# Four 32-partition transposes of mixer B's diagonal blocks made into one 128-partition transpose, before and after the substitution

## The chip, the cores and the metric

The kernel runs on one core of a Trainium2 chip. The metric is device time in microseconds of one execution, as the median of several runs. All arithmetic of this kernel is in 32-bit floats.

## What is computed

The program is one inference step of a two-layer hybrid backbone for 128 context tokens and 1024 latent tokens. Layer 0 has windowed attention (mixer A) beside a bidirectional RWKV-7 recurrence (mixer B), layer 1 has differential attention (mixer C). The change lies in mixer B alone. Its recurrence, for each of 8 heads and both directions, is

```python
def rwkv_scan(S0, r, decay, kk, a, k, v, reverse):
    def step(S, inp):
        r_t, w_t, kk_t, a_t, k_t, v_t = inp
        sa = jnp.einsum('bhvk,bhk->bhv', S, -kk_t)
        S = (S * w_t[:, :, None, :] + sa[..., None] * (kk_t * a_t)[:, :, None, :]
             + v_t[..., None] * k_t[:, :, None, :])
        return S, jnp.einsum('bhvk,bhk->bhv', S, r_t)
    ...
```

The kernel does not step through tokens. It cuts the sequence into chunks of 64 tokens. Inside a chunk the term with `sa` couples each token to the earlier ones, which makes a unit triangular 64x64 system; its inverse is needed before the chunk's state update can be done with matrix products.

## The kernel before

**Items.** Mixer B's work is cut into nine items (`items`): two halves of the latent tokens for each of four pairs of heads, and one item for the context tokens of all heads. An item holds 32 triangular systems of 64x64: two directions, eight chunks and two heads. Of each system the matrix `za` is stored with partitions as rows. Along the free axis lie 16 systems (`units`, index `u`), and an index `a` (0 or 1) tells the two chunks of a pair apart, one of which lies on the lower and one on the upper 64 partitions.

**Inverse.** A 64x64 triangular matrix is seen as four 32x32 blocks. The two diagonal blocks are inverted by substitution (`b_subst`), the off-diagonal block then follows from two small matrix products (`b_invert`). The 128 partitions hold four groups `g` of 32 partitions; group `g` holds a diagonal block that begins at column `32 * (g % 2)`, so groups 0 and 2 have it at column 0 and groups 1 and 3 at column 32.

- `b_subst` first turns each diagonal block, so that columns of all systems lie side by side (`mp`, 128 x 32 x 32), with one VectorE transpose per group (L1032, four of 32 x 1024, each element written twice). Then GpSimd does 31 steps of a multiplication (L1039, into `tmp`) and an addition (L1041, into `rp`). `rp` starts as the identity, loaded by a DMA on SP's queue (L1028).
- `b_invert` turns `rp` back into `Rt` with four VectorE transposes (L1050, 32 x 512), turns the first diagonal block once more into `rt11` (an `hb` buffer) with two transposes (L1056, 32 x 512), and then TensorE multiplies (L1061: `hb` by `za` into `sc`; ScalarE L1063 copies the result; L1068 multiplies by `Rt`; ScalarE L1070 copies into `Rt`). With `Rt` complete, TensorE makes `pa` (L1082), VectorE scales it to `E` (L1086), and L1096 and ScalarE L1099 prepare `VU`.

**Scan.** `b_scan` steps through eight chunk positions of an item, and each step waits for the one before: TensorE L1139 (`E` by `G`), VectorE L1141 (`VU`), TensorE L1143, VectorE L1150 (`G`, two instructions), ScalarE L1152 (`S`).

**Pipeline over items.** One turn of the loop over `items` (a stage here) does, interleaved, the scan of item i, the inverse of item i+1, the front part of item i+2 in both directions (`b_front`: TensorE L988, L998, L1013; VectorE `za` L1004 and `q` L1006), the substitution of item i+2 near the end, and the preparation of item i+3 (`b_prep`: VectorE L930 to L954, ScalarE L921 to L957, TensorE L914). The modulation of later parts (`mod_chunks`: TensorE L287 and L293, ScalarE L289) fills in. In every second stage the finish of a pair of heads is added (`b_finish`, L1176 to L1206). `timeline` sets when each of them is issued, and

```python
            timeline((scan, 8, *t[0]), (invert(i + 1), 8, *t[1]), (done, 10, *t[2]),
                     (front(i + 2, 0), 12, *t[3]), (prep(i + 2, 1), 5, *t[4]), (front(i + 2, 1), 12, *t[5]),
                     (subst(i + 2), 2, *t[6]), (prep(i + 3, 0), 5, *t[7]), (some(mod, t[8]), max(t[8], 1), *t[9]))
```

from that order a scheduler with costs of its own makes one fixed order for each engine. Every engine runs its instructions in that order, and an instruction that waits holds up all behind it. `mp`, `rp` and `Rt` exist once; `hb` is a ring of eleven buffers. `behind` only adds an order, that `Rt` is written after the neighbours' last use, and no wait.

Of the kernel before, what the change touches and what calls it, by code (L numbers as in the profile page):

```python
# [19 lines left out]
P = 128  # L20
# [121 lines left out]
def hybrid_step(ctx: ExitStack, tc: tile.TileContext, I, O, stop=99):  # L142
    nc = tc.nc
    PE, VE, AE, GE, SP = nc.tensor, nc.vector, nc.scalar, nc.gpsimd, nc.sync
    def behind(ins, others):

        for o in others:
            if o is not None:
                tc.add_manual_dep(ins.ins, o.ins.name, mybir.DependencyInfo(
                    mybir.DependencyClass.NoSync, mybir.DependencyReason.DATA), reason="order")  # L150

    def space(name, bufs, **kw):
        return tc.tile_pool(name=name, bufs=bufs, reuse_waits="tile", **kw)
# [3 lines left out]
    def tl(pool, shape, tag, dt=F32, bufs=None):  # L157
        uid[0] += 1
        kw = {} if bufs is None else {"bufs": bufs}
        return pool.tile(list(shape), dt, tag=tag, name=f"{tag}_{uid[0]}", **kw)  # L160
# [679 lines left out]
    ON_VE = ()  # L840
# [35 lines left out]
    low, high = (lambda j: slice(64 * j, 64 * j + 32)), (lambda j: slice(64 * j + 32, 64 * j + 64))  # L876
# [141 lines left out]
    def units(it):  # L1018
        return [it.za[:, a].rearrange("p d x h t -> p (d x h) t") for a in range(2)]

    def b_subst(it, pre, eye, eng):

        mp, rpb = tl(pre, [P, 32, 32], "mp"), tl(pre, [P, 16, 32], "rp")
        tmp = tl(pre, [P, 136], "tmp")
        za = units(it)
        SP.dma_start(rpb.rearrange("p t i -> p (t i)"), eye)  # L1028
        for g in range(4):
            s = slice(32 * g, 32 * g + 32)  # L1030
            m = za[1 - g // 2][s, :, 32 * (g % 2):32 * (g % 2) + 32].rearrange("p u c -> p c u")
            VE.transpose(mp[s].rearrange("p c i -> p (c i)"),  # L1032
                         m.rearrange("p c (o u) -> p c o u", o=1).to_broadcast([32, 32, 2, 16]))
        yield
        for j in range(31, 0, -1):
            t = j // 2
            n = 16 - t
            tv = tmp[:, :n * j].rearrange("p (t i) -> p t i", i=j)
            eng.tensor_tensor(tv, mp[:, j:j + 1, 0:j].to_broadcast([P, n, j]),  # L1039
                             rpb[:, t:16, j:j + 1].to_broadcast([P, n, j]), ALU.mult)  # L1040
            eng.tensor_tensor(rpb[:, t:16, 0:j], rpb[:, t:16, 0:j], tv, ALU.add)  # L1041
        it.rpb = rpb

    def b_invert(it, Rt, pool, pre, ps_s, ps_a):

        rpb, za = it.rpb, units(it)
        for g in (0, 2, 1, 3):
            s = slice(32 * g, 32 * g + 32)
            o = 32 * (g % 2)
            behind(VE.transpose(Rt[s, :, o:o + 32].rearrange("p u (c o) -> p c o u", o=2),  # L1050
                                rpb[s].rearrange("p c i -> p (c i)")),
                   [getattr(n, "tail", None) for n in it.near])
        it.free = True
        rt11, v1 = hb(pool, [P, 16, 32]), hb(pool, [P, 16, 32])
        for e in range(2):
            VE.transpose(rt11[low(e)], Rt[low(e), :, 0:32])  # L1056
        yield
        pv = tl(ps_s, [P, 16, 32], "sc")
        for u in range(16):
            for e in range(2):  # L1060
                PE.matmul(pv[high(e), u], za[1 - e][low(e), u, 32:64], rt11[low(e), u], start=True, stop=True)  # L1061
        for e in range(2):
            AE.copy(v1[high(e)], pv[high(e)])  # L1063
        yield
        pv = tl(ps_s, [P, 16, 32], "sc")
        for u in range(16):
            for e in range(2):
                PE.matmul(pv[low(e), u], v1[high(e), u], Rt[high(e), u, 32:64], start=True, stop=True)  # L1068
        for e in range(2):
            AE.copy(Rt[low(e), :, 32:64], pv[low(e)])  # L1070
        yield
        De = tl(pre, [P, 2, 8], "De")
        VE.memset(De, -0.5)
        w = 1 if it.nl == 1 else 2
        VE.tensor_scalar(De[:, :, 1:8:w], it.D[:, :, 0:7:w], -0.5, None, op0=ALU.mult)

        it.E = tl(pool, [P, 2, 8, 64], "E", bufs=2)
        pe = tl(ps_a, [P, 2, 2, 4, 64], "pa")
        for d in range(2):
            for x in range(4):  # L1080
                for h, e in ((0, 0), (1, 1), (0, 1), (1, 0)):
                    PE.matmul(pe[half_of(h), e, d, x], it.zn[half_of(e), d, x, half_of(h)],  # L1082
                              Rt[half_of(e), 8 * d + 2 * x + h], start=True, stop=True)
            yield
        for e in range(2):
            VE.tensor_tensor(it.E[:, :, e:8:2].rearrange("p d x t -> p (d x) t"),  # L1086
                             pe[:, e].rearrange("p d x t -> p (d x) t"),
                             De[:, :, 1 - e:8:2].rearrange("p d (x o) -> p (d x) o", o=1).to_broadcast([P, 8, 64]),
                             ALU.mult)
        yield  # L1090
        for d in range(2):
            pt = tl(ps_s, [P, 4, 2, 64], "sc")
            for x in range(4):
                for h in range(2):
                    for e in range(2):
                        PE.matmul(pt[half_of(e), x, h], Rt[half_of(e), 8 * d + 2 * x + h],  # L1096
                                  it.av[half_of(e), d, x, half_of(h)], start=True, stop=True)
            for e in range(2):
                AE.copy(it.VU[half_of(e), :, d, 1 - e], pt[half_of(e)].rearrange("p x h v -> p x (h v)"))  # L1099
            yield  # L1100
# [109 lines left out]
    with ExitStack() as ph2:  # L1210
        bc = ph2.enter_context(space("bc", 1))
        pool = ph2.enter_context(space("bpool", 1))
# [5 lines left out]
        pre = early.enter_context(space("bpre", 1))  # L1218
# [4 lines left out]
        hb = lambda pl, shape: tl(pl, shape, "hb", bufs=NHB)  # L1223
        ones, cen, ma = load_cst(bc, "ones", "cen", "ma")
        eye = I["cst"][:, CST["eye"][0]:sum(CST["eye"])]
        ind = ones[:, 0:P:64]
        Rt = tl(pre, [P, 16, 64], "Rt")
# [14 lines left out]
        items = []  # L1242
# [30 lines left out]
            return b_front(items[i], d, pool, pre, ps_y, ps_a, ma) if i < len(items) else None  # L1273

        def subst(i):
            return b_subst(items[i], pre, eye, VE if i in ON_VE else GE) if i < len(items) else None

        def invert(i):
            if not 0 <= i < len(items):
                return None  # L1280
            items[i].near = [items[j] for j in (i - 1, i + 1) if 0 <= j < len(items)]
            return b_invert(items[i], Rt, pool, pre, ps_s, ps_a)
# [22 lines left out]
        for i in range(-2, len(items)):  # L1305
            scan, tail = None, None
            if i == -1:
                blk.__exit__(None, None, None)
            if i >= 0:
                it = items[i]  # L1310
                scan = scan_all(it)
                tail = b_finish(it, pool, ps_s, ones, cen, ind) if it.last else None
# [25 lines left out]
            if i + 1 == len(items):  # L1338
                timeline((after(scan, tail), 21, 0, 1), (some(outs, 9), 9, *T8))
                continue  # L1340
# [3 lines that stand above are left out]
            done = tail  # L1344
    if stop <= 2:
# [442 lines left out]
```

## Time and profile before

| what | value |
|---|---|
| median of three runs | 2371.25 us (2370.67 to 2379.9) |
| the profiled execution | 2364.72 us, span 2362.9 us |
| mean granted TensorE clock | 0.919 |
| mixer B's items in the trace | first `mp` transpose at 609.9 us, last `Rt` transpose at about 1221 us |
| DVE line L1032, 36 transposes | 69.6 us busy, 1934 ns each |
| DVE line L1050, 36 transposes | 37.8 us busy, 1049 ns each |
| DVE line L1056, 18 transposes | 12.6 us busy, 701 ns each |
| POOL lines L1039 and L1041, 279 each | 128.0 and 133.8 us busy |

The page gives the busy time of each engine, the same in 40 slices, and groups of instructions. A row of the timeline gives the start, the duration, engine, line, operation, output and inputs, the count, and in brackets how long the engine stood still before it and what ended the wait. A row of the windows gives, for a stretch of time, the busy time of each engine with its instructions, then the clock granted to TensorE (1 is full speed), the share of the DMA engines and GB/s.

### The profile page before, as it was taken

How to read it: one execution, taken by the hardware profiler on the slowest of the kernel's cores; microseconds unless marked ns; L12 is line 12 of the kernel's file. 1: busy time of each engine (PE TensorE's matmuls, PEld its weight loads, DVE VectorE, ACT ScalarE, POOL GpSimd, SP SyncE). 2: the span in 40 equal slices, each digit the busy share in tenths (PEclk: the TensorE clock that was granted, in tenths of full speed). 3: DMA queues.
4: the chain of work that ended last, by engine and by line, in shares of the span. 5: the costliest groups of instructions: out<-in, count | busy, mean ns of one | idle time of the engine just before them, and what ended most of it. 6: DMA issues, size and time to landing. Idle time of an engine off the chain costs nothing. (4 is left out here: it accounts for less than half of the span.)

```text
span 2362.9 us, 40947 instructions
## 1 busy us (share of the span) xinstructions
PE 2109.9 (89%) x15258; PEld 1864.3 (79%) x15258; DVE 1556.2 (66%) x3838; ACT 1044.5 (44%) x2808; POOL 644.1 (27%) x897
## 2 busy tenths in 40 slices
PE   7899989997578888987899789999999999998798
PEld 4899988996456666776677678899989899997676
DVE  4445555445566676775755985778887878887743
ACT  3433334333343343352434445545555565555621
POOL 0222212310433344542240431222222122211212
PEclk9999999998877887795889899999999999999799
DMA  6421213102543243333145533011010100101233
GB/s 262 138 74 65 79 53 111 64 32 92 156 124 96 83 133 113 118 115 87 62 141 185 187 135 104 19 34 35 18 52 23 31 27 26 40 13 59 72 105 116
DMA packets 164648, 205.73 MB, mean 87 GB/s; under 512 B 16193, under 2 KB 107745, under 8 KB 164449
## 3 DMA queue, kind: packets, MB, share of 16 engines
q1 hardware_dynamic: 161584, 198.25, 26.5%
q10 hardware_dynamic: 2864, 4.85, 0.6%
q8 instruction: 121, 1.98, 0.4%
q14 instruction: 79, 0.64, 0.1%
HBM read 152.32 MB, written 50.74 MB: 86 GB/s over the span
## 5 line engine op out<-in xcount | busy, mean ns | idle before, releaser
L1493 ACT ACTIVATE p<-s,mx 128x384 f32<-128x384 f32 (+1 forms) x400 | 224.8, 571 | 128.3 <-DVE mx L1490 105.1
L1488 DVE TENSOR_REDUCE mc<-s 128x1 f32<-128x384 f32 x384 | 205.3, 551 | 37.0 <-PE s L1486 33.3
L1039 POOL TENSOR_TENSOR tmp<-mp,rp 128x126 f32<-128x126 f32 (+22 forms) x279 | 128.0, 459 | 342.6 <-DVE mp L1032 281.6
L352 PE MATMUL ps<-wch,hh 128*128 128x384 f32 x576 | 207.2, 361 | 15.3 <-DVE hh L1638 13.8
L1486 PE MATMUL s<-kst,qs 128*128 128x384 f32 x768 | 203.0, 365 | 18.6 <-ACT p L1493 17.9
L353 PE MATMUL ps<-wcl,hh 128*128 128x384 f32 x576 | 199.7, 347 | 5.1 <-POOL wcl L261 5.1
L354 PE MATMUL ps<-wch,hl 128*128 128x384 f32 x576 | 198.1, 344 | 3.0 <-DVE hl L1639 2.7
L366 PE MATMUL ps<-hh,wgh 128*128 128x384 f32 x504 | 174.6, 347 | 5.8 <-DVE bo L234 5.6
L367 PE MATMUL ps<-hl,wgh 128*128 128x384 f32 x504 | 173.7, 345 | 0.0
L368 PE MATMUL ps<-hh,wgl 128*128 128x384 f32 x504 | 172.8, 343 | 0.0
L399 POOL TENSOR_TENSOR q<-ropea,ropeb 128x256 f32<-128x256 f32 x56 | 42.9, 766 | 450.8 <-DVE ropeb L396 285.1
L1486 PEld LDWEIGHTS s<-kst,qs 128*128 128x128 f32 x768 | 131.2, 196 | 37.2 <-ACT p L1493 29.9
L261 POOL TENSOR_TENSOR wgl<-raw,wgh 128x1024 fp32r<-128x1024 f32 (+1 forms) x37 | 72.9, 1971 | 277.3 <-ACT wgh L260 261.9
L1041 POOL TENSOR_TENSOR rp<-rp,tmp 128x126 f32<-128x126 f32 (+22 forms) x279 | 133.8, 480 | 21.9
L352 PEld LDWEIGHTS ps<-wch,hh 128*128 128x128 f32 x576 | 111.1, 193 | 21.0 <-issue 12.1
L1370 DVE TENSOR_TENSOR al<-pt,ah 128x512 fp32r<-128x512 f32 (+2 forms) x168 | 100.7, 615 | 36.9 <-ACT ah L1369 35.6
L1369 ACT CAST ah<-pt 128x512 fp32r<-128x512 f32 (+2 forms) x168 | 86.4, 533 | 83.4 <-PE pt L1524 82.8
L353 PEld LDWEIGHTS ps<-wcl,hh 128*128 128x128 f32 x576 | 111.2, 193 | 7.6 <-POOL wcl L261 6.9
L354 PEld LDWEIGHTS ps<-wch,hl 128*128 128x128 f32 x576 | 110.7, 192 | 5.2 <-DVE hl L1639 4.8
L261 POOL TENSOR_TENSOR wcl<-raw,wch 128x512 fp32r<-128x512 f32 x48 | 63.3, 1327 | 161.3 <-ACT wch L260 161.3
L1524 PE MATMUL pt<-cst,p 128*128 128x128 f32 x584 | 98.4, 283 | 8.6 <-DVE p L1506 4.3
L366 PEld LDWEIGHTS ps<-hh,wgh 128*128 128x128 f32 x504 | 96.5, 192 | 7.9 <-DVE bo L234 6.2
(411 smaller groups left out, 5927.4 us busy)
## 6 DMA issues: line engine op xcount, KB each, us to landing
hb<-pbT SPq DMA_DIRECT2D x90, 256.0 KB, 4.4
adaw<-in_ada_w_dram SPq DMA_DIRECT2D x64, 256.0 KB, 3.4
raw<-in_wc_dram SPq DMA_DIRECT2D x48, 256.0 KB, 2.8
adaw<-in_ada_w_dram SPq DMA_DIRECT2D x8, 1024.0 KB, 11.9
pbT<-bm SPq DMA_DIRECT2D x16, 512.0 KB, 2.7
low<-lowT SPq DMA_DIRECT2D x16, 512.0 KB, 4.8
raw<-in_wo_dram SPq DMA_DIRECT2D x32, 256.0 KB, 2.8
raw<-in_wpb_dram SPq DMA_DIRECT2D x13, 512.0 KB, 3.5
```

The costliest lines, as they stand in the source:

```text
L261: eng.tensor_tensor(lo[:, j:j + w], raw[:, :w], hi[:, j:j + w].bitcast(F32), ALU.subtract)
L352: PE.matmul(ps[:, :n], hh[:, k, s], wh[:, k], start=k == 0, stop=False)
L353: PE.matmul(ps[:, :n], hh[:, k, s], wl[:, k], start=False, stop=False)
L354: PE.matmul(ps[:, :n], hl[:, k, s], wh[:, k], start=False, stop=k == KT - 1)
L366: PE.matmul(ps[:, :THIRD], wh[:, k], hh[:, k, s], start=k == 0, stop=False)
L367: PE.matmul(ps[:, :THIRD], wh[:, k], hl[:, k, s], start=False, stop=False)
L368: PE.matmul(ps[:, :THIRD], wl[:, k], hh[:, k, s], start=False, stop=k == KT - 1)
L1039: eng.tensor_tensor(tv, mp[:, j:j + 1, 0:j].to_broadcast([P, n, j]), rpb[:, t:16, j:j + 1].to_broadcast([P, n, j]), ALU.mult)
L1041: eng.tensor_tensor(rpb[:, t:16, 0:j], rpb[:, t:16, 0:j], tv, ALU.add)
L1486: PE.matmul(s[c][:, :w], qs[:, e, z], hd.kp[:, z] if own else hd.kst[:, z, w * c:w * c + w], start=e == 0, stop=e == 1)
L1488: VE.tensor_reduce(mc[:, c:c + 1] if nb > 1 else mx, s[c][:, :w], axis=AX.X, op=ALU.min)
L1493: AE.activation(e[:, w * c:w * c + w], s[c][:, :w], AF.Exp, scale=-1.0, bias=mx, accum_out=sums[:, z, c:c + 1])
```

## The change

`b_subst` gets the item's buffer pool and takes one more `hb` buffer, `dg`. Four copies on the engine of the substitution (GpSimd for every item, as `ON_VE` is empty) bring the four diagonal blocks to column 0; one VectorE transpose of 128 x 1024 then makes `mp`. `b_invert` turns all of `rp` with one VectorE transpose of 128 x 512 into columns 32 to 63 of `Rt`, makes `rt11` with one transpose over all partitions, and lets ScalarE copy the first diagonal block from there to columns 0 to 31 on the two groups that have it. Line numbers behind this place fall by three (L1061 becomes L1058, L1139 becomes L1136 and so on).

```diff
-    def b_subst(it, pre, eye, eng):
+    def b_subst(it, pool, pre, eye, eng):
...
+        dg = hb(pool, [P, 16, 32])
         for g in range(4):
             s = slice(32 * g, 32 * g + 32)
-            m = za[1 - g // 2][s, :, 32 * (g % 2):32 * (g % 2) + 32].rearrange("p u c -> p c u")
-            VE.transpose(mp[s].rearrange("p c i -> p (c i)"),
-                         m.rearrange("p c (o u) -> p c o u", o=1).to_broadcast([32, 32, 2, 16]))
+            eng.tensor_copy(dg[s], za[1 - g // 2][s, :, 32 * (g % 2):32 * (g % 2) + 32])
+        VE.transpose(mp.rearrange("p c i -> p (c i)"),
+                     dg.rearrange("p (o u) c -> p c o u", o=1).to_broadcast([P, 32, 2, 16]))
...
-        for g in (0, 2, 1, 3):
-            s = slice(32 * g, 32 * g + 32)
-            o = 32 * (g % 2)
-            behind(VE.transpose(Rt[s, :, o:o + 32].rearrange("p u (c o) -> p c o u", o=2),
-                                rpb[s].rearrange("p c i -> p (c i)")),
-                   [getattr(n, "tail", None) for n in it.near])
-        it.free = True
+        behind(VE.transpose(Rt[:, :, 32:64].rearrange("p u (c o) -> p c o u", o=2), rpb.rearrange("p c i -> p (c i)")),
+               [getattr(n, "tail", None) for n in it.near])
         rt11, v1 = hb(pool, [P, 16, 32]), hb(pool, [P, 16, 32])
+        VE.transpose(rt11.rearrange("p u c -> p (u c)"), Rt[:, :, 32:64])
         for e in range(2):
-            VE.transpose(rt11[low(e)], Rt[low(e), :, 0:32])
+            AE.copy(Rt[low(e), :, 0:32], Rt[low(e), :, 32:64])
```

The scheduler also gives the work around it another order. Three places follow. The first is VectorE's order for item 2's `Rt` (from `rp_7102`) and item 3's `mp` (`mp_7779`); `VU` and `G` are scan steps, `za` and `q` belong to the front of item 3, `E` to the inverse of item 2. Before:

```order
L1050 STREAM_TRANSPOSE Rt_5573<-rp_7102 32x32x16 x4
L1056 STREAM_TRANSPOSE hb_7502<-Rt_5573 32x512 x2
L978 SCALAR_TENSOR_TENSOR hb_7508<-hb_7438,rkh_5536,hb_7304 128x512
L1141 TENSOR_TENSOR VU_6017<-VU_6017,sc_7520 64x2x128
...
L1006 TENSOR_TENSOR q_1300_7506<-pa_7678,cstones_5571 128x2x4x64
L1141 TENSOR_TENSOR VU_6017<-VU_6017,sc_7733 64x2x128
L1032 STREAM_TRANSPOSE mp_7779<-za_7327 32x1024 x2
L1150 TENSOR_TENSOR G_957_5576<-S_960_5579,sc_7733 64x2x64 x2
L1122 TENSOR_TENSOR y_6602<-y_6602,yb_7519 128x256 x2
L1032 STREAM_TRANSPOSE mp_7779<-za_7327 32x1024 x2
L1086 TENSOR_TENSOR E_7698<-pa_7699,De_7695 128x8x64
```

With the change:

```order
L1048 STREAM_TRANSPOSE Rt_5573<-rp_7102 128x32x16
L1138 TENSOR_TENSOR VU_6019<-VU_6019,sc_7520 64x2x128
L1051 STREAM_TRANSPOSE hb_7501<-Rt_5573 128x512
L978 SCALAR_TENSOR_TENSOR hb_7508<-hb_7440,rkh_5536,hb_7310 128x512
...
L1006 TENSOR_TENSOR q_1303_7506<-pa_7678,cstones_5571 128x2x4x64
L1138 TENSOR_TENSOR VU_6019<-VU_6019,sc_7733 64x2x128
L1033 STREAM_TRANSPOSE mp_7779<-hb_7783 128x1024
L1147 TENSOR_TENSOR G_957_5576<-S_960_5579,sc_7733 64x2x64 x2
L1119 TENSOR_TENSOR y_6604<-y_6604,yb_7519 128x256 x2
L1083 TENSOR_TENSOR E_7698<-pa_7699,De_7695 128x8x64 x2
```

The scan's `VU` has moved ahead of the `rt11` transpose, and the whole `mp` transpose, which now waits for GpSimd's copies, stands ahead of the scan's `G`.

The second is TensorE's order at the inverse of the same item 2 (`sc_7540` is its first product, `sc_7520` a scan step, `py_7584` modulation, `pa_7575` the front of item 3). Before:

```order
L998 MATMUL pa_7575<-zr_1286_7393,kbt_7396 128x128 x4
L287 MATMUL py_7584<-adaw_7580,sc_64 2x128 x4
L287 MATMUL py_7584<-adaw_7582,sc_64 2x128 x4
L998 MATMUL pa_7575<-zr_1286_7393,kbt_7396 128x128
L1061 MATMUL sc_7540<-hb_7502,za_6648 32x32
L998 MATMUL pa_7575<-zr_1286_7393,kbt_7396 128x128 x2
L1061 MATMUL sc_7540<-hb_7502,za_6648 32x32 x31
L998 MATMUL pa_7575<-zr_1286_7393,kbt_7396 128x128
L1143 MATMUL sc_7520<-VU_6017,kb_1062_6022 128x128
```

With the change:

```order
L998 MATMUL pa_7575<-zr_1289_7395,kbt_7398 128x128 x4
L1140 MATMUL sc_7520<-VU_6019,kb_1063_6024 128x128
L1140 MATMUL sc_7520<-VU_6019,kb_1101_6188 128x128
L1058 MATMUL sc_7540<-hb_7501,za_6650 32x32 x32
L287 MATMUL py_7584<-adaw_7580,sc_64 2x128 x4
L287 MATMUL py_7584<-adaw_7582,sc_64 2x128 x4
L998 MATMUL pa_7575<-zr_1289_7395,kbt_7398 128x128 x4
```

The scan's product stands first now, and the eight modulation products that stood ahead of the inverse stand behind it.

The third is VectorE's order at item 0's `mp`, where nothing is scanned yet (L930 to L954 prepare item 1):

```order
-L1032 STREAM_TRANSPOSE mp_5917<-za_5648 32x1024 x4
 L930 TENSOR_SCALAR hb_5908<-hb_5908 128x512
-L934 MEMSET hb_5987 128x8
+L934 MEMSET hb_5989 128x8
 L301 TENSOR_SCALAR gcol_77<-py_5914,prm_60 128x2
...
+L954 TENSOR_TENSOR kbt_5997<-hb_6001,hb_5908 128x4x2x64
+L1033 STREAM_TRANSPOSE mp_5917<-hb_5921 128x1024
```

Here the transpose has moved behind the instructions that prepare item 1, L930 to L954. On GpSimd each item's four copies stand right ahead of its substitution; nothing else moves there. The order of layer 1 is the same as before on every engine.

More of the change, by code (lines that the diff above doesn't have):

```diff
@@ L1275, in subst @@
         def subst(i):
-            return b_subst(items[i], pre, eye, VE if i in ON_VE else GE) if i < len(items) else None
+            return b_subst(items[i], pool, pre, eye, VE if i in ON_VE else GE) if i < len(items) else None
         def invert(i):
```

## Prediction

> **What bounds the kernel now.** I read the page first.
>
> ```profile
> span 2362.9 us, 40947 instructions
> ...
> PE 2109.9 (89%) x15258; PEld 1864.3 (79%) x15258; DVE 1556.2 (66%) x3838; ACT 1044.5 (44%) x2808; POOL 644.1 (27%) x897
> ...
> PEclk9999999998877887795889899999999999999799
> ```
>
> TensorE (PE) is busy 89% of the span, so elsewhere a faster VectorE (DVE) is worth nothing. But slices 10 to 21, of 59 us each, are mixer B, and there the granted clock falls to 0.7 and 0.5. So I read that part apart, from 590 to 1260 us: first the groups of the changed lines, then the waits.
>
> ```profile
> L1032 DVE STREAM_TRANSPOSE mp<-za 32x1024 f32<-32x1024 f32 x36 | 69.6, 1934 | 0.4
> ...
> L1050 DVE STREAM_TRANSPOSE Rt<-rp 32x512 f32<-32x512 f32 x36 | 37.8, 1049 | 42.3 <-POOL rp L1041 41.6
> ...
> L1056 DVE STREAM_TRANSPOSE hb<-Rt 32x512 f32<-32x512 f32 x18 | 12.6, 701 | 0.5
> ...
> L1063 ACT COPY hb<-sc 32x512 f32<-32x512 f32 x18 | 10.4, 577 | 46.0 <-PE sc L1061 45.8
> ```
>
> ```profile
> POOL tmp L1039 <- DVE mp L1032: 281.6, 8, 39.9
> ...
> DVE Rt L1050 <- POOL rp L1041: 41.6, 5, 18.5
> ...
> PE sc L1061 <- DVE hb L1056: 32.5, 8, 8.1
> ```
>
> GpSimd (POOL) starts its substitution when `mp` is done; DVE then waits for its last addition (41.6 us, five times) and PE for the `rt11` transpose (32.5 us, eight times). So POOL, 27% busy over all, sits in a ring: `mp`, substitution, `Rt`, `rt11`, PE, `za`, `mp`. The timelines show one turn, from item 2's `Rt` to item 3's substitution; first DVE.
>
> ```profile
> 789.71 4.21 DVE L1050 STREAM_TRANSPOSE Rt<-rp 32x512 f32<-32x512 f32 x4 [6.30 <-POOL rp L1041]
> 793.95 1.43 DVE L1056 STREAM_TRANSPOSE hb<-Rt 32x512 f32<-32x512 f32 x2
> ...
> 813.81 0.75 DVE L1004 TENSOR_TENSOR za<-pa,cstones 128x256 f32<-128x256 f32 x2
> ...
> 815.08 0.40 DVE L1141 TENSOR_TENSOR VU<-VU,sc 64x256 f32<-64x256 f32 x1
> 815.41 3.93 DVE L1032 STREAM_TRANSPOSE mp<-za 32x1024 f32<-32x1024 f32 x2
> 819.35 0.58 DVE L1150 TENSOR_TENSOR G<-S,sc 64x128 f32<-64x128 f32 x2
> ...
> 820.75 3.93 DVE L1032 STREAM_TRANSPOSE mp<-za 32x1024 f32<-32x1024 f32 x2
> ```
>
> Then PE and POOL:
>
> ```profile
> 784.78 1.91 PE L287 MATMUL py<-adaw,sc 128*2 128x128 f32 x16
> 786.61 0.49 PE L998 MATMUL pa<-zr,kbt 64*128 64x128 f32 x2
> 794.70 0.31 PE L1061 MATMUL sc<-hb,za 32*32 32x32 f32 x2 [7.60 <-DVE hb L1056]
> ...
> 798.23 1.22 PE L1143 MATMUL sc<-VU,kb 128*128 128x128 f32 x4
> ...
> 812.36 0.71 PE L1143 MATMUL sc<-VU,kb 128*128 128x128 f32 x4
> ```
>
> ```profile
> 789.15 0.22 POOL L1039 TENSOR_TENSOR tmp<-mp,rp 128x16 f32<-128x16 f32 x1
> 789.45 0.23 POOL L1041 TENSOR_TENSOR rp<-rp,tmp 128x16 f32<-128x16 f32 x1
> 824.81 0.24 POOL L1039 TENSOR_TENSOR tmp<-mp,rp 128x31 f32<-128x31 f32 x1 [35.14 <-DVE mp L1032]
> ```
>
> POOL ends at 789.68, `Rt` and `rt11` take 5.7 us, PE resumes at 794.70 after 7.60 us, `za` ends at 814.56, `mp` at 824.68, 10.1 us behind it. POOL stood 35.14 us. Whatever shortens `za` to `mp`, or POOL to PE, shortens the turn if nothing else ends last. I put the nine items in two classes. Items 1, 2, 4 and 6 are like this one (POOL ends, DVE waiting). At items 3, 5 and 7 a pair's finish fills DVE and PE as well.
>
> **`mp`.** Four transposes of 1.93 us leave, one comes, of the same free length on 128 partitions. All 36 rows of its line have 32 partitions, so the trace bounds a transpose of 128 only from 1.93 us (partitions side by side) to 7.7 us (one after another, which would undo the change). In the rows above `VU` takes 0.40 us with 64x256 and the two `za` of 128x256 take 0.75, so DVE's time goes by the free length and not by the partitions; I take 1.93. Ahead stand four POOL copies of 512 elements on 32 partitions, an operation the trace doesn't have. The nearest rows:
>
> ```profile
> L1240 POOL MEMSET rmask<- 128x512 f32 x1 | 0.5, 524 | 0.0
> ...
> L261 POOL TENSOR_TENSOR wcl<-raw,wch 128x512 fp32r<-128x512 f32 x48 | 63.3, 1327 | 161.3 <-ACT wch L260 161.3
> ```
>
> A copy reads one input, a memset none and the subtraction two. With 0.08 us between POOL instructions (789.15 + 0.22 is 789.37, the next starts at 789.45), four cost 2.4 us by the memset and 5.6 by the subtraction. I take 0.62 each, near the memset, so 2.8; with 1.94 for the transpose and 0.2 for handing over, `za` to `mp` becomes 5.0 us (4.5 to 7.7). Its value before, by the start of `za` and the end of `mp`, for items 1 and 7 at the ends of the spread:
>
> ```profile
> 678.46 0.76 DVE L1004 TENSOR_TENSOR za<-pa,cstones 128x256 f32<-128x256 f32 x2 [0.92 <-PE pa L998]
> ...
> 679.73 7.63 DVE L1032 STREAM_TRANSPOSE mp<-za 32x1024 f32<-32x1024 f32 x4
> ...
> 1092.96 0.76 DVE L1004 TENSOR_TENSOR za<-pa,cstones 128x256 f32<-128x256 f32 x2
> ...
> 1103.52 3.88 DVE L1032 STREAM_TRANSPOSE mp<-za 32x1024 f32<-32x1024 f32 x2
> ```
>
> That is 8.1 and 13.7 us; the same reading gives 9.2, 10.1, 10.4, 12.6, 9.2 and 10.5 for items 2 to 6 and 8, of which 7.7 is transposes and the rest `G`, `y` and `E` between them. The whole transpose stands ahead of these now. So items 1, 2, 4, 6 gain 36.9 − 20.0 = 16.9 us, items 3 and 5 gain 22.7 − 10.0 = 12.7. Item 7's inverse is reached late, after POOL has long ended, so of its 8.7 I count 4; item 8's last stage is PE's, 1 of 5.5.
>
> [...]
>
> **`Rt` and `rt11`.** 4.21 + 1.43 us become 1.05 + 0.70, and PE can be 3.9 us earlier on paper. The order takes it back in the first class: the eight L287 products and the L998, in which PE worked until 787.1, stand behind the inverse now, and the scan's `VU` and L1140 stand ahead. PE's work is the same, PE is idle until POOL ends either way, and the moved products (half of the sixteen L287 that took 1.91, and 0.49) lengthen the path to `za` by 1.4, more at the low clock, while `Rt`, `VU` and `rt11` together take 2.2 us where 5.7 stood, 3.5 less, of which the scan's product L1140, now ahead, takes some 0.7 to 1.2 (L1143). What is left, about 1 us, is within what PE's own order can give or take; I count 0 for these four, bounds −2 to +2 each. In the second class `VU` stood behind it all:
>
> ```profile
> 860.56 1.07 DVE L1050 STREAM_TRANSPOSE Rt<-rp 32x512 f32<-32x512 f32 x1
> ...
> 867.18 0.42 DVE L1141 TENSOR_TENSOR VU<-VU,sc 64x256 f32<-64x256 f32 x1
> ...
> 867.66 0.71 PE L1143 MATMUL sc<-VU,kb 128*128 128x128 f32 x4 [2.23 <-DVE VU L1141]
> ```
>
> PE's 2.23 us go, and what is late next is PE's own work; three such stages give 6.9, say 7. ScalarE's two added copies (0.58 each, by L1063) run while it waits for L1061 (45.8 us): nothing; were that cover gone, 1.2 us an item, as L1065 (L1068 before) needs `Rt` complete. L1028's DMA on SP waits for the readers of the buffers as before, none of it moved past another queue; the `dg` buffer takes one of eleven `hb` slots, and I see no wait for one.
>
> **Item 0.** Its `mp` stands behind the preparation of item 1 now:
>
> ```profile
> 609.88 7.71 DVE L1032 STREAM_TRANSPOSE mp<-za 32x1024 f32<-32x1024 f32 x4
> 617.62 0.43 DVE L930 TENSOR_SCALAR hb<-hb 128x512 f32<-128x512 f32 x1
> ...
> 622.73 0.77 DVE L954 TENSOR_TENSOR kbt<-hb,hb 128x512 f32<-128x512 f32 x1
> ```
>
> L930 to L954 take 5.9 us. From 609.9, `mp` ends at 617.7 with these and its own 1.93, against 617.6, and later if one of them waits where now it doesn't: up to 3 us. POOL then makes DVE wait the full 18.5 us for `Rt`. I count −2 (−3 to +1).
>
> **Sum.** 16.9 + 12.7 + 4 + 1 + 7 − 2 = 39.6, say 40 us: 2364.72 of the profiled execution becomes 2325. The median of the runs shown is 6.5 above that execution, so I forecast 2371.25 − 40 = 2331. With all bounds at once: copies at 5.6 take 8 × 2.8 = 22 from it, the −2 four times 8 more, item 0 one more, leaving 9; the good ends (copies 3, `Rt` 8, item 0 3, item 7 5) make 59. This case's own range is 2312, with all the good ends, to 2347, with half of the bad ones.
>
> **Rivals.** *B, the clock comes back too.* The stretches of item 2's turn:
>
> ```profile
> 747.30:815.40 68.10, 54.98 (x653) 44.58 (x652) 42.81 (x77) 26.16 (x71) 29.14 (x62) 0.82 0.33 98
> ...
> 788.00:792.00 4.00, 0.00 (x0) 0.00 (x0) 2.23 (x3) 0.00 (x0) 1.28 (x6) 0.88 0.04 11
> 796.00:800.00 4.00, 4.00 (x67) 3.37 (x64) 1.77 (x6) 1.15 (x2) 0.00 (x0) 0.50 0.94 267
> ```
>
> PE stood through 788 to 792 and right after had a clock of 0.50, at which L1143 took 1.22 us against 0.71. A stage of 68 us at 0.82 loses 68 × 0.18 = 12 us of full clock; if a good third of it, 4.4 us, came back in each of eight stages, 35 us more: 2296. Against it: the second class fell to half speed behind a wait of only 2.23 us, so a short wait is no cure, and the first class's idle still reaches until POOL ends, whose wait stays.
>
> [...]
>
> *C, PE's fixed order is late next.* PE is busy 54.98 of those 68.10 us, so a turn cannot lose more than 13 us without PE's being the end of it, and PE's order was made for other durations than these. If its rows for the next front come 2.6 us later than I think in eight stages, half of the 40 us is eaten: 2352. For it speaks item 8, where PE is the end already; against it, that I count 5 us a turn, well under 13.
>
> *D, no change in time.* `mp` comes earlier but POOL stood 35 us anyway and `Rt` is taken when the scan gets there. Against: DVE waited for POOL at five items. 2366 to 2371.
>
> *E, slower: DVE stands at `mp` for the copies, with `G` behind it.* Before, `G` started at 819.35, between the transposes. Now it starts at 814.56 + c + 0.2 + 1.94, c being the four copies. It is later from c = 2.65 on, just at my value; the scan then loses, though the ring gains. The scan decides only if it, not POOL, ends the stage. With c = 5.6 it is 3.0 us a stage, 24 in eight: 2395.
>
> **Numbers.** A 0.60, B 0.15, C 0.14, D 0.06, E 0.05. This kernel's measurement tells about 0.5%, 12 us, from no change; A, B and C are below 2359, so faster 0.89, same 0.06 (D), slower 0.05 (E). For 8 in 10 the range leaves D, E and the tails of B and C out: 2290 to 2360.
>
> **What the profile after would show.** Right: copies of 0.5 to 0.75 us on POOL, one `mp` transpose of 1.93 us ending 5 us behind `za`, one `Rt` of 1.05, `VU` no longer behind `rt11` at items 3, 5 and 7, and first `mp` to last `Rt` 40 us shorter with the substitution itself the same 31 to 34 us. Wrong: copies over 1.3 us (E), a transpose over 2 us, PE idle of another name at the same places (C), windows with a clock over 0.9 (B), or POOL's wait for `mp` longer by what `mp` saved (D).

## The result, and the profile after

The changed kernel takes 2277.45 us (median of four runs, 2272.26 to 2279.24) against 2374.24 for the kernel before: ratio 0.9587, interval 0.9559 to 0.9614. Measured again beside later experiments it was 2273.65 and 0.9561 (0.9541 to 0.9580). The forecast was 2331, its range 2290 to 2360. The sign was right; the gain is some 97 us where 40 were forecast.

The page of the changed kernel, profiled at 2272.26 us:

```profile
span 2270.5 us, 40971 instructions
...
PE 2054.4 (90%) x15258; PEld 1818.9 (80%) x15258; DVE 1468.0 (65%) x3775; ACT 1057.8 (47%) x2826; POOL 662.9 (29%) x933
...
PEclk9999999999878998987998989999999999998899
```

PE has the same 15258 matmul records (each product left two: the 32 of L1058 at an item's inverse are x64 below) and 55 us less busy time: the same work ran at a higher clock (0.944 in the mean, 0.919 before). The slices of mixer B, which fell to 0.7 and once to 0.5, now stand at 0.7 to 0.9. The changed lines, as groups from 590 to 1170 us (busy time and mean ns, then the idle time ahead of them):

```profile
L1032 POOL COPY hb<-za 32x512 f32<-32x512 f32 x36 | 21.8, 606 | 178.3 <-DVE za L1004 132.9 <-issue 26.4 <-ACT S L1149 17.9
L1033 DVE STREAM_TRANSPOSE mp<-hb 128x1024 f32<-128x1024 f32 x9 | 17.6, 1961 | 9.1 <-POOL hb L1032 9.0
...
L1053 ACT COPY Rt<-Rt 32x512 f32<-32x512 f32 x18 | 11.1, 615 | 44.2 <-DVE Rt L1048 26.1 <-DVE hb L934 17.3 <-DVE rsy L252 0.5
...
L1048 DVE STREAM_TRANSPOSE Rt<-rp 128x512 f32<-128x512 f32 x9 | 9.5, 1058 | 47.3 <-POOL rp L1042 47.3
L1051 DVE STREAM_TRANSPOSE hb<-Rt 128x512 f32<-128x512 f32 x9 | 6.4, 710 | 0.2
```

A transpose of 128 partitions takes as long as one of 32 did (1961, 1058 and 710 ns against 1934, 1049 and 701), and a copy 0.61 us. Waits in the same stretch:

```profile
POOL hb L1032 <- DVE za L1004: 132.9, 7, 22.2
...
DVE Rt L1048 <- POOL rp L1042: 47.3, 5, 22.0
...
PE sc L1140 <- DVE VU L1138: 29.8, 12, 7.6
...
POOL tmp L1040 <- DVE mp L1033: 25.1, 7, 12.6
```

POOL waits for `za` now, 132.9 us in seven turns (178.3 us in all ahead of its copies, the group above), and 25.1 us more for `mp` behind the copies, where it waited 281.6 for `mp`; VectorE still waits for POOL at five items, and PE waits for the scan's `VU`, which stands behind `Rt`, where it waited for `rt11`. The same turn as in the prediction, item 2's `Rt` to item 3's `mp`, on DVE, POOL and PE:

```profile
770.97 1.04 DVE L1048 STREAM_TRANSPOSE Rt<-rp 128x512 f32<-128x512 f32 x1 [6.30 <-POOL rp L1042]
...
772.50 0.71 DVE L1051 STREAM_TRANSPOSE hb<-Rt 128x512 f32<-128x512 f32 x1
...
787.69 0.76 DVE L1004 TENSOR_TENSOR za<-pa,cstones 128x256 f32<-128x256 f32 x2
...
790.91 1.98 DVE L1033 STREAM_TRANSPOSE mp<-hb 128x1024 f32<-128x1024 f32 x1 [1.54 <-POOL hb L1032]
```

```profile
770.71 0.23 POOL L1042 TENSOR_TENSOR rp<-rp,tmp 128x16 f32<-128x16 f32 x1
788.33 2.55 POOL L1032 COPY hb<-za 32x512 f32<-32x512 f32 x4 [17.39 <-DVE za L1004]
792.97 0.24 POOL L1040 TENSOR_TENSOR tmp<-mp,rp 128x31 f32<-128x31 f32 x1 [2.09 <-DVE mp L1033]
```

```profile
772.52 1.22 PE L1140 MATMUL sc<-VU,kb 128*128 128x128 f32 x4 [6.41 <-DVE VU L1138]
773.67 1.92 PE L1058 MATMUL sc<-hb,za 32*32 32x32 f32 x64
775.52 2.92 PE L287 MATMUL py<-adaw,sc 128*2 128x128 f32 x16
...
779.01 0.71 PE L1136 MATMUL sc<-G,E 128*128 128x128 f32 x4
```

From `za`'s end to the substitution is 4.6 us where it was 10.3. And the first products behind the wait are at half clock (L1140 takes 1.22 us) as before, but the products from 779 on are at full clock (1.00 from 779 to 788), where before they stayed at half until 812 (0.52 from 798 to 812). The windows from `Rt` to the next `za`, before and after (PE busy, its clock third from the end of the row):

```profile
789.71:814.56 24.85, 19.42 (x208) 15.84 (x208) 11.67 (x23) 6.28 (x17) 0.00 (x0) 0.59 0.25 75
```

```profile
770.97:788.33 17.36, 15.38 (x225) 12.55 (x225) 7.48 (x18) 8.17 (x22) 0.00 (x1) 0.81 0.21 62
```

7.5 us shorter with 17 PE instructions more, at a clock of 0.81 instead of 0.59.

Read the same way for all nine items, the ring adds up as follows. "Mp" is from `za`'s end to `mp`'s end (items 1 to 8), "substitution" from there to the start of `Rt` (0 to 8), "Rt" from there to the first product of the inverse (0 to 7), "front" from there to the end of the next `za` (0 to 7), all in us; "half" is the time at a clock of 0.5 within the fronts, by the trace's records of the granted clock. The ratio is to the kernel before, with its interval. Each row is one profiled execution, and the clock differs between executions: the ten of x_fill20 run from 2339.91 us (mean clock 0.939) to 2360.46 us (0.924), and its profiled one, 2358.40, lies near the top.

| kernel | ratio | mp | substitution | Rt | front | half |
|---|---|---|---|---|---|---|
| before | 1 | 83.9 | 317.3 | 52.5 | 145.5 | 105.1 |
| changed | 0.9587 (0.9559 to 0.9614) | 45.8 | 310.2 | 29.4 | 121.5 | 27.4 |
| e1_subst | 0.9879 (0.9843 to 0.9915) | 49.4 | 311.9 | 57.6 | 147.0 | 115.4 |
| e2_invert | 0.9764 (0.9720 to 0.9809) | 77.9 | 319.6 | 27.6 | 123.3 | 25.2 |
| x_fill20 | 0.9925 (0.9895 to 0.9955) | 80.4 | 317.1 | 62.3 | 138.4 | 75.0 |
| x_fill50 | 0.9894 (0.9860 to 0.9928) | 78.0 | 320.6 | 63.4 | 112.8 | 13.9 |
| x_rows32 | 1.0011 (0.9992 to 1.0030) | 78.0 | 323.6 | 91.3 | 114.0 | 16.6 |
| x_cols2 | 0.9865 (0.9827 to 0.9903) | 79.2 | 317.8 | 61.8 | 125.3 | 42.6 |
| a_fill | 0.9548 (0.9521 to 0.9574) | 45.9 | 307.3 | 30.1 | 117.1 | 11.4 |
| e4_copy8 | 0.9669 (0.9638 to 0.9701) | 66.7 | 311.3 | 29.4 | 123.5 | 28.5 |
| v_split | 0.9545 (0.9521 to 0.9569) | 37.9 | 317.2 | 29.1 | 124.3 | 31.3 |
| v_all | 0.9510 (0.9488 to 0.9532) | 38.0 | 316.0 | 31.3 | 116.1 | 8.5 |
| after_again | 0.9561 (0.9541 to 0.9580) | 45.9 | 309.8 | 29.4 | 122.2 | 30.5 |
| m_late | 0.9621 (0.9564 to 0.9677) | 48.9 | 318.6 | 25.7 | 123.5 | 28.3 |

Before against changed: 38.1 + 7.1 + 23.1 + 24.0 = 92.3 us, less 2.7 that the first `mp` ends later, is the 89.6 by which the last `Rt` starts earlier (1216.8 to 1127.2) and nearly all of the 92.4 between the two spans. So there are three things to explain: `mp` (38), `Rt` (23) and the front (24), in which nothing was taken away and 78 us of half clock are gone. The substitution's 7 lie at items 0 and 7 (3.5 and 5.3); at item 7 `Rt` now starts 3.0 us after POOL's end, where it started 7.4 us after it.

### The profile page after: what moved, and what is told of

Same layout as the page of the kernel before. It is cut to its first block, busy times and chain, and to the rows that moved or that the text cites. A ratio compares the mean times of both kernels' runs of the same rounds, so it can differ in the third digit from the quotient of the medians.

```text
span 2270.5 us, 40971 instructions
## 1 busy us (share of the span) xinstructions
PE 2054.4 (90%) x15258; PEld 1818.9 (80%) x15258; DVE 1468.0 (65%) x3775; ACT 1057.8 (47%) x2826; POOL 662.9 (29%) x933
## 3 DMA queue, kind: packets, MB, share of 16 engines
q1 hardware_dynamic: 161584, 198.25, 27.4%
## 5 line engine op out<-in xcount | busy, mean ns | idle before, releaser
L1040 POOL TENSOR_TENSOR tmp<-mp,rp 128x126 f32<-128x126 f32 (+22 forms) x279 | 125.8, 451 | 56.2 <-DVE mp L1033 25.1
```

## The experiments

**Each side alone.** e1_subst has the change in `b_subst` and the old `b_invert`; e2_invert the other way round. The orders show that the products behind the inverse are rearranged by the inverse's side only: e1_subst keeps the old order there, e2_invert has that of the changed kernel.

```diff
 e1_subst: before, with
+            eng.tensor_copy(dg[s], za[1 - g // 2][s, :, 32 * (g % 2):32 * (g % 2) + 32])
+        VE.transpose(mp..., dg...)
 e2_invert: before, with
+        behind(VE.transpose(Rt[:, :, 32:64]..., rpb...), ...)
+        VE.transpose(rt11..., Rt[:, :, 32:64])
+            AE.copy(Rt[low(e), :, 0:32], Rt[low(e), :, 32:64])
```

> Only the substitution's side of the change: four copies on GpSimd and one transpose for mp; Rt and rt11 stay as before, with the old order there. Theory R (the ring: each part is worth the time that it takes out of the way from za to mp and from POOL's end to the inverse, and the clock adds to the second only): za to mp falls from 83.9 us in sum over items 1 to 8 to some 46, Rt to inverse stays 52, the stretches from the inverse to the next za stay near 145 with over 80 us of half clock in them: 38 us faster than before, ratio 0.984. Rival P (the parts work together: a shorter ring alone already brings the clock back): the half clock in those stretches falls below 50 us and the time by over 55 us, ratio below 0.977.

> Only the inverse's side: one Rt transpose, one rt11 transpose, two ScalarE copies; mp as before. Theory R: Rt to inverse falls from 52.5 us in sum over items 0 to 7 to some 30, and the stretch from inverse to za from 145 to some 122 because the clock comes back (half clock there from 105 to under 50 us): 45 us faster, ratio 0.981. My prediction's reading (what PE's order takes back cancels it): 7 us, ratio 0.997. Theory P (only both together free the clock): the transposes alone, 23 us, ratio 0.990.

e1_subst gains 1.2%, 29 us, and e2_invert 2.4%, 56 us. In e1_subst `mp` falls to 49.4 where 46 was forecast, `Rt` and the front do not fall, and the half clock stays (115 us). In e2_invert `Rt` falls by 25, the front by 22 and its half clock from 105 to 25 us. So rival P is out: a shorter ring alone does not bring the clock back. My prediction's 7 us for the inverse's side is out as well. Theory R has the parts right; its times, 38 and 45 us, are 9 us too high and 11 us too low. The two gains, 33 and 51 us by the ring (first `mp` to last `Rt`), leave 8 of the changed kernel's 92 to their working together. PE at item 2's inverse in e1_subst and in e2_invert:

```profile
789.41 0.31 PE L1062 MATMUL sc<-hb,za 32*32 32x32 f32 x2 [8.13 <-DVE hb L1057]
790.38 1.91 PE L1062 MATMUL sc<-hb,za 32*32 32x32 f32 x62
...
792.94 1.22 PE L1144 MATMUL sc<-VU,kb 128*128 128x128 f32 x4
```

```profile
788.41 1.22 PE L1139 MATMUL sc<-VU,kb 128*128 128x128 f32 x4 [6.43 <-DVE VU L1137]
789.56 1.92 PE L1057 MATMUL sc<-hb,za 32*32 32x32 f32 x64
791.40 3.25 PE L287 MATMUL py<-adaw,sc 128*2 128x128 f32 x16
```

Both waits are long (8.13 and 6.43 us) and both starts are at half clock (the scan's product takes 1.22 us in both, 0.71 at full clock). In e1_subst it lasts 21.0 us of this front, in e2_invert 4.6. So it isn't the length of the wait that differs, but what stands behind it.

**Filling the wait.** Unread products are put on PE ahead of the wait, for items 1, 2, 4 and 6. `FILL` gives their number, and they are ordered behind a late step of the substitution.

```diff
+        if it.fill:
+            pf = tl(ps_s, [P, 512], "sc")
+            for n in range(it.fill):
+                behind(PE.matmul(pf[:, 0:P], ident, ident, start=True, stop=True), [it.late])
```

> The kernel before, and 20 products of 128x128 that nobody reads, put on PE ahead of the wait for the inverse of items 1, 2, 4 and 6. The scheduler then gives PE the order of the changed kernel there (the scan's product first, the L287 products behind the inverse). 20 products take 3.6 us of a wait that I put at 11 us in this order, so over 5 us of wait remain. This is the control for the next kernel, which has the same order. Theory C (the wait decides the clock): half clock behind these four inverses stays about 76 us in sum, time within 0.7% of before. Theory O (the order of the products behind the wait brings the clock back): half clock there below 40 us, 10 to 20 us faster.

> The same with 50 products, 8.9 us: the wait of items 1, 2, 4 and 6 is filled but for some 2 us. Theory C (an idle PE loses the clock, so a filled wait keeps it): half clock behind these four inverses falls from 76 us in sum to below 20, and the kernel is 15 to 28 us faster than with 20 products, though it does more and the ring is as long. Rival O (the mix of products behind the wait decides): half clock as with 20 products, time the same within 5 us or slower by the added work.

With 20 products (4.73 us at item 2, where 3.6 was expected) the wait there is still 7.57 us, and the clock falls to 0.50; but with the changed kernel's order behind it, it comes back after two windows (6.8 us behind each of three of these inverses, 8.2 behind the fourth, where the kernel before had 17 to 21). That part of theory C was wrong, and theory O right: half clock there is 29 us in sum, and these four fronts are 14 us shorter. (Item 5's front, whose wait is not filled, is 7 us longer, with 17.2 us of half clock where the kernel before had none; why isn't shown.) `Rt` is 10 us longer, because the scan's product now stands ahead of the inverse and waits behind the four old transposes, so the ring is as long as before (598 and 599 us); the 0.75% of its ratio is not explained by it. With 50 products (11.43 us at item 2, where 8.9 was expected) no half clock is left behind these inverses, three of their fronts take 13.7 us where they took 16.7, and the added products cost nothing: the ring is 23 us shorter than with 20, the profiled spans differ by 14.7 us and the medians by 10 (2343.04 and 2353.18, with overlapping intervals of the ratio), which is at or under the low end of what C expected. About half of it is not the filling's own: of the 25.6 us by which the fronts are shorter, 13.1 lie at the four filled items and 12.6 at items 3 and 5, which are not filled and whose half clock (15.6 and 17.2 us with 20 products) is gone. So both act: a filled wait keeps the clock, and the order behind a wait brings it back.

**What keeps the clock.** The clock is granted in steps of 3.41 us in these traces: of the 76 records of it before and the 66 with the change all but the last of each, at the end of the program, last a whole multiple of 3.413 us, the shortest one such step, and each grants 1.00 or 0.50. For all such windows of six traces in mixer B (before, changed, e1_subst, e2_invert, x_fill20, x_fill50) I asked what in a window goes with the clock of the next. After a full window, 112 of 826 fell, and PE's busy time sorts 96% of them right (saying that none falls sorts 86%). After a half window, 113 of 351 came back, and busy time sorts no better than saying that none comes back (68%), but the columns streamed, each times the rows that its product uses as a share of 128, sort 89%, with the same bound in both directions (about 1500 such columns a window; the 0.72 in the expectation below is on a scale that it does not give). The eight other traces bear the bound out: at 1500 it sorts 97% of their 1210 full windows and 87% of their 361 half windows, where saying that nothing changes sorts 89% and 62%. That is still a correlation, so x_rows32 and x_cols2 repeat x_fill50 with products of 32 rows and of 2 columns.

```diff
-                behind(PE.matmul(pf[:, 0:P], ident, ident, start=True, stop=True), [it.late])
+x_rows32:      behind(PE.matmul(pf[:, 0:P], ident[0:32], ident[0:32], start=True, stop=True), [it.late])
+x_cols2:       behind(PE.matmul(pf[0:2, 0:P], ident[:, 0:2], ident, start=True, stop=True), [it.late])
```

> The kernel with 50 unread products ahead of the four inverses, in the same order and of the same length (128 columns streamed), but each on 32 rows of the array where the last one used 128. Over the windows of six traces, the clock that follows went best with the streamed columns weighted by the share of rows in use (a bound of about 0.72 in both directions). Theory W (row-weighted work decides): PE is just as busy through the wait, yet the clock is lost: half clock behind the inverses of items 1, 2, 4, 6 from 0 to over 20 us in sum, and 5 to 15 us slower than with 128 rows. Rival I (only idle time decides): half clock stays 0 and the time that of the 128-row kernel, ratio 0.989.

> The same again, but 128 rows and 2 columns of the array in use. Theory W by rows: as good as 128 by 128, half clock 0 behind the four inverses, ratio to before 0.989. Rival W by area (rows times columns): as bad as 32 rows or worse, half clock over 20 us.

The filling products in x_fill50, x_rows32 and x_cols2 (two records each), and 4 us windows inside them:

```profile
783.76 11.43 PE L1055 MATMUL sc<-cst 128*128 128x128 f32 x100
```

```profile
788.00:792.00 4.00, 4.00 (x38) 4.00 (x37) 0.76 (x1) 0.00 (x0) 2.50 (x10) 1.00 0.00 0
792.00:796.00 4.00, 4.00 (x39) 4.00 (x37) 3.89 (x5) 0.33 (x2) 0.00 (x0) 1.00 0.00 0
```

```profile
789.56 17.02 PE L1055 MATMUL sc<-cst 32*128 32x128 f32 x100
```

```profile
788.00:792.00 4.00, 4.00 (x51) 3.75 (x50) 1.45 (x5) 1.07 (x3) 3.29 (x10) 1.00 0.01 4
792.00:796.00 4.00, 4.00 (x33) 4.00 (x32) 0.00 (x0) 0.00 (x0) 3.22 (x11) 0.84 0.00 0
796.00:800.00 4.00, 4.00 (x21) 4.00 (x21) 2.87 (x3) 0.00 (x0) 0.80 (x4) 0.50 0.00 0
```

```profile
779.26 11.08 PE L1055 MATMUL sc<-cst 128*2 128x128 f32 x100
```

```profile
784.00:788.00 4.00, 4.00 (x40) 3.11 (x38) 1.26 (x2) 0.00 (x0) 2.05 (x8) 1.00 0.00 0
```

PE is busy for 4.00 of 4.00 us in every row, yet with 32 rows its clock falls to 0.50 in the middle of the stretch, and the same 100 records take 17.0 us instead of 11.4. With 128 rows and 2 columns it holds 1.00. Theory W by rows is what the runs show: rival I, idle time alone, is out, and so is area. One part of the expectation missed its place: with 32 rows the half clock lies in the products themselves (11 to 13 us in each of the four) and not behind the inverse, so it is `Rt` that grows by 28 us; the whole is 1.2% slower than with 128 rows (1.0011 against 0.9894), 28 us where 5 to 15 were expected. And x_cols2 lost the clock again behind two of the four inverses, 13.6 us of half clock where 0 was expected. At item 2 PE waited 1.62 us there behind the filling, against 1.50 in x_fill50, and the window with the wait held 1312 row-weighted columns against 1664 in x_fill50, which kept its clock: one below the bound, one above.

**The products behind the wait.** m_late moves the L287 products, which use 128 rows, from behind L1058 to behind L1065, by the times of the modulation (three entries of `TIMES`; two have the first edit).

```diff
-(-0.1, 1.05)   +(0.6, 1.05)      and    -12, (0, 1)   +12, (0.6, 1.0)
```

> The changed kernel with the modulation's interval moved to the later part of each stage, so that in the first class of items (2, 4 and 6 at the least) the L287 products, which use 128 rows of the array, no longer stand directly behind the inverse but some 8 us later, behind L1065; the rest of the order there stays. Theory W (behind the wait the clock comes back in the first window with enough row-weighted work, and L287 is what made it enough): half clock between the inverse and the next za of items 2, 4 and 6 rises from 4 to 7 us each to 10 or more, and that stretch does not get shorter although 2 to 3 us of L287 have left its front. Rival (the clock comes back by itself in two windows whatever runs, or the scan's product standing first does it): half clock there stays under 7 us and the stretch becomes 2 us shorter. The whole time is no test here, since the modulation also moves against the rest of the stage.

At item 2 it went as theory W has it: the half clock lasts 13.7 us where the changed kernel had 4.0, it ends as the L287 products do, and the front is 19.3 us instead of 14.8. PE there:

```profile
770.39 0.71 PE L1140 MATMUL sc<-VU,kb 128*128 128x128 f32 x4 [1.42 <-DVE VU L1138]
...
771.45 1.92 PE L1058 MATMUL sc<-hb,za 32*32 32x32 f32 x64
...
774.87 1.22 PE L1136 MATMUL sc<-G,E 128*128 128x128 f32 x4
...
782.63 3.10 PE L287 MATMUL py<-adaw,sc 128*2 128x128 f32 x16
...
786.90 0.71 PE L1136 MATMUL sc<-G,E 128*128 128x128 f32 x4
```

The three windows of 3.41 us behind the fall held 1136, 1264 and 1168 row-weighted columns with PE busy throughout; the fourth, with the L287 products, held 1920, and then the clock came back. At items 4 and 6 the expectation failed: no clock was lost behind the inverse there, and the fronts were 13.4 us. The modulation's times also moved everything ahead of the wait, and PE's wait ahead of the inverse had shrunk to 0.89 and 0.78 us there, so no lost clock was left to bring back. This run speaks for W at one place and says nothing at the other two.

**Is the ring the bound?** e4_copy8 doubles the copies.

```diff
-        for g in range(4):
+        for g in (0, 1, 2, 3) * 2:
```

> The changed kernel with the four copies done twice: 2.5 us more in each of nine turns, with the same order on VectorE and TensorE. Theory R (the ring is the bound): eight turns, item 7 less since POOL waits there anyway: 15 to 20 us slower than the changed kernel, ratio to before 0.966 to 0.968. Rival 1 (copies lie beside other work): under 5 us, ratio below 0.962. Rival 2 (VectorE stands at mp with the scan's G behind it, rival E of the prediction): more than the added time, over 25 us, ratio over 0.970.

```profile
L1032 POOL COPY hb<-za 32x512 f32<-32x512 f32 x72 | 45.5, 632 | 190.7 <-DVE za L1004 123.6 <-ACT S L1149 35.9 <-DMA hb<-pbT 27.8
```

23.7 us more of copies make `mp` 21 us longer and the kernel 0.8% (19 us) to 1.1% (26 us) slower, against the two measurements of the changed kernel. About one for one, as theory R has it. At items 1, 2, 4 and 6 `Rt` still starts as POOL ends, so POOL and not the scan ends those turns; rival E of the prediction, in which the scan does, isn't seen.

**Better versions.** a_fill is the changed kernel with 30 unread products in the waits of items 1, 2, 4 and 6, v_split shares the copies with ScalarE, v_all has both.

```diff
-            eng.tensor_copy(dg[s], za[1 - g // 2][s, :, 32 * (g % 2):32 * (g % 2) + 32])
+            m = za[1 - g // 2][s, :, 32 * (g % 2):32 * (g % 2) + 32]
+            eng.tensor_copy(dg[s], m) if g % 2 else AE.copy(dg[s], m)
```

> The changed kernel, with 30 unread products of 128x128 (5.3 us) ahead of the inverses of items 1, 2, 4 and 6, in a wait of 6.4 us. Theory W: the half clock left behind these four inverses (22 us of 27) goes, and the kernel gains up to half of it: 5 to 11 us on the changed kernel, ratio to before 0.954 to 0.957. Rival: those rows are no longer what ends the ring there, or the products delay the scan: no change or slower, ratio 0.959 to 0.965.

> The changed kernel with two of the four copies on ScalarE, side by side with the two on GpSimd. Theory R (the ring is the bound at one for one; doubling the copies cost some 18 us): za to mp falls from 4.4 to 3.2 us in seven turns, 7 to 9 us faster than the changed kernel, ratio to before 0.955 to 0.956. Rival: ScalarE is held by what stands ahead of its copies (S waits for VectorE's G), so the copies start later: no change or slower, ratio 0.959 or more.

> The changed kernel with the split copies and the 30 unread products of 128 rows in the four waits. Both gains add in theory R: 10 for the products and 8 for the copies, 18 us faster than the changed kernel, ratio to before 0.951. Rival: with a shorter ring TensorE's own work ends the turns and the second gain is lost, ratio 0.955.

> The changed kernel itself, on the same chip as the two versions: ratio to before 0.959, and the ring as in its first profile.

a_fill: 2266.52 us, ratio 0.9548, 7 to 11 us under the two medians of the changed kernel, with an interval that overlaps theirs. Behind three of the four inverses no half clock is left; the filling (6.96 us where 5.3 was expected), the scan's product and the inverse (L1067 here) at item 2, all at full clock (1.00 from 766 to 782):

```profile
765.95 6.96 PE L1056 MATMUL sc<-cst 128*128 128x128 f32 x60
...
775.38 0.71 PE L1149 MATMUL sc<-VU,kb 128*128 128x128 f32 x4 [0.85 <-DVE VU L1147]
776.13 1.20 PE L1067 MATMUL sc<-hb,za 32*32 32x32 f32 x64
```

v_split shortens `mp` by 8 us as expected, but the substitution's end waits 9 us longer for `Rt` at items 3, 7 and 8, where DVE comes to `Rt` after POOL has ended (3.7, 6.0 and 6.7 us, against 0, 2.3 and 5.2 in after_again), and the substitution's column grows by 7: 2270.57 against 2273.65 for the changed kernel beside it, with overlapping intervals. The forecast of 7 to 9 us was too high, since most of it moves into stages that POOL does not end; a gain from the split copies alone is not shown. v_all is the fastest, 2261.70 us, 0.9510 as forecast, and clear of the changed kernel on the same chip (0.9561): 12 us faster, where 18 were expected.

## Why the prediction was wrong

By the terms of its sum (us; forecast, then measured between the two profiles):

| term | forecast | measured |
|---|---|---|
| `mp`, items 1, 2, 4, 6 | 16.9 | 36.9 − 17.5 = 19.4 |
| `mp`, items 3, 5 | 12.7 | 22.7 − 8.8 = 13.9 |
| `mp`, items 7 and 8 | 4 + 1 | −1.4 + 6.1 |
| `Rt` and `rt11`, with what they bring PE | 7 | 23.1 + 24.0 = 47.1 |
| item 0's `mp` | −2 | −2.7, and 3.5 back in its substitution |

- **The `mp` term was right.** The copies took 0.61 us where I took 0.62, the transpose 1.96 where I took 1.93, `za` to `mp` 4.4 us where I had 5.0. No row showed such a copy, only 0.52 and 1.33 us at the two sides, so that 0.62 came this close is partly luck. At item 7 `mp` stands behind the preparation, where DVE stood 4.44 us for ScalarE's L924, and nothing was gained; that items 7 and 8 together come to 4.7 for 5 is luck.
- **The step that failed is "I count 0 for these four".** It said that PE's new order takes back what the transposes save, because the moved products lengthen the path. It priced these products at a clock that stays as it was. (It also took only half of the row's sixteen L287 records as moved; they are the eight products, two records each, so 2.4 us moved by that row's time and not 1.4, which would have made the step's "about 1 us" about 0.) They did lie on the path (2.92 us for L287), but the front became 5.1 us shorter at item 2, because behind them the clock was full (1.00 from 779 to 788). e2_invert shows it without the change of `mp`: the front 22 us shorter at 80 us less of half clock.
- **The direct part was mis-sized too.** `Rt` to the first product fell by 23.1 us in eight items: 1.6 to 2.3 at items 1, 2, 4 and 6 (5.0 to 2.7 at item 2, with the scan's product in between), 4.1 at item 7 and 7.2 at item 0, which I had left out. For items 3 and 5 the 2.3 each was right (7.9 to 5.7).
- **Rival B was named, with the wrong mechanism.** The prediction looked for the clock in the length of the waits, and gave B 0.15 and 35 us. The wait is still 6.41 us and the clock still falls (0.50 from 772.5 to 775.5). What changed is how soon it returns. The row against B in the prediction (a clock lost behind a wait of 2.23 us; it was 0.56 from 867 to 890) should have sent me to look at what PE ran there: L287 and small products, and then 32-row products for many windows. Nor was B's price enough: 2296 is still above the 2277 measured, since the direct part was low as well. With 23 for it instead of 7, and the fronts' 24, the sum of 40 becomes 80, and the 7 us that the substitution's column fell make 87.
- **C, D and E did not occur.** PE's order was no hindrance, POOL's wait for `mp` did not grow, and doubling c cost one for one, with `Rt` still starting as POOL ends (e4_copy8).

Nor does idle time alone account for the clock. It fell behind the waits of 6.41 to 8.13 us at item 2, but x_rows32's windows, busy 4.00 of 4.00 us, stand at 0.50: what counts as work there goes by the rows in use. And at m_late's item 2 it fell behind a wait of only 1.42 us.

What stays open: the exact measure of work (89% of the returns are sorted by it, not all), why items 3 and 5 keep or lose the clock from kernel to kernel, and 8 us that the two sides gain together.

## What to carry to other kernels

A transpose took as long on 128 partitions as on 32 here (1961 and 1934 ns for the free length of 1024, 1058 and 1049 for 512), so bringing blocks to one offset with four copies of 0.61 us paid, in a ring that waits for it (`mp` 38 us shorter over eight turns); price it turn by turn, from the end of one engine's work to the start of the next. Before counting a reordered product as a cost on the path, look at the clock in that stretch: where PE runs at half speed behind a wait, wide-row products put there can cost less than nothing (2.92 us of L287 at item 2, and a front 5.1 us shorter), and narrow ones (32 rows) can keep or even bring the half clock with PE busy all the time (0.50 in x_rows32, busy 4.00 of 4.00 us). Where a wait must stay, a few unread 128-row products in it are worth a try (here 7 to 11 us by the medians for 120 of them, with overlapping intervals), and enough of them: behind a rest of 1.50 us the clock was kept (x_fill50, item 2), behind one of 1.62 us it was lost (x_cols2, item 2).

## What the runs showed of the hardware

- TensorE's granted clock changed in steps of 3.41 us and fell from 1.00 to 0.50 while PE was busy without a gap, when the products used 32 of 128 rows (100 records in 17.0 us instead of 11.4). With 128 rows and only 2 columns it stayed at 1.00.
- The bound lay at about 1500 row-weighted columns a window in both directions (it sorts 89% of 351 half windows in six traces, and in eight others 97% of 1210 full and 87% of 361 half ones). From the 11.43 us of 100 records, a window holds an estimated 30 records of 128 columns at full clock: 30 × 128 × 1/4 = 960 with 32 rows, 3800 with 128 rows.
- VectorE's transposes took the same time on 128 partitions as on 32 (1961 and 1934 ns).
- GpSimd's copy of 32x512 took 606 ns, ScalarE's of the same size 615 (L1053).
